# Decayed B and K from a column per chunk, and corner clears and decay diagonals on GpSimd, in a two-layer gated encoder

## The chip, the core and the metric

The kernel runs on one core of a Trainium2 chip. The metric is device time in microseconds from the launch to the end of the program; smaller is better. The core's engines work side by side, each through its own queue in a fixed order: TensorE (PE, with its weight loads as PEld), VectorE (DVE), ScalarE (ACT), GpSimd (POOL), and SyncE (SP), which issues most transfers.

## The reference

Two layers of an encoder with 512 tokens of width 1024 in float32. Each layer projects the normalised input, runs five mixers on parts of the projection, merges their outputs through gates, projects again and normalises. The change lies in one mixer, a recurrence with 8 heads of 64, run forward and backward (e = 0 and 1):

```python
def rwkv7_step(state, inp):
    r, w, k, v, a, bb = inp
    sa = jnp.einsum('bhij,bhj->bhi', state, a)
    state = state * w[:, :, None, :] + sa[..., None] * bb[:, :, None, :] + v[..., None] * k[:, :, None, :]
    return state, jnp.einsum('bhij,bhj->bhi', state, r)
...
    for e, rev in ((0, False), (1, True)):
        ke = k * (1.0 + (a[:, :, e] - 1.0) * k_a)
        be = kk * a[:, :, e]
        xs = (rh, seq_heads(decay[:, :, e]), seq_heads(ke), vh, ah, seq_heads(be))
        _, ye = lax.scan(rwkv7_step, jnp.zeros((b, B_HEADS, HEAD_DIM, HEAD_DIM), F32), xs, reverse=rev)
        ys.append(ye)
```

`decay` is exp of a negative number for each channel and token, so products of decays over a stretch are exp of differences of a running sum.

## The kernel before

**Stages.** An opening part normalises the input. Each layer then has attention mixers, the recurrence, and an end with the last branch of the merge, the output projection and the normalisation. The merge (`branch_steps`, five branches of eight column blocks) consists of long chains of 512-column matmuls. The part of it whose inputs are ready is used as filler: `pull` advances it by one step at each `yield` of the recurrence. Inputs of later branches come back from DRAM into four buffers `o`, by transfers that GpSimd issues (line 366).

**The recurrence** treats the 512 tokens as 8 chunks of 64. A unit is a pair of heads in one direction; there are 8 units in a layer (p = 0 to 3, e = 0 and 1). A unit has an `early` part, which has no link to the state, and a `late` part, which passes the state from chunk to chunk. The loop at the end runs `late` of unit n beside `early` of unit n + 1, and after a pair's backward unit its `finish`.

`early` (line 804 on): a scan (line 820) makes the running sum `csum` of the log decay within each chunk. `tot` is its last column in each chunk, and `gc`, 8 columns, is the decay over a whole chunk. Line 825 makes `bef`, the sum before the token; lines 826 and 827 make `aft`, what remains after it. The forward direction takes `incl, excl, comp` as `csum, bef, aft`, the backward one as their mirror. From the inclusive sum come B and K divided by the decay so far; they lie in `BK` (lines 852 and 853), grouped by halves, and go with A and R into the score matmuls of line 881. Line 908 takes the exponential of `comp`, the decay from a token to its chunk's end. Lines 910 and 912 multiply B (`ai`) and K (`ke`) by it; four transposes each (line 921) and copies by ScalarE (line 927) bring them into `OM`. Line 933 writes, for each head, eight diagonal 64x64 blocks with `gc` on the diagonal into `A0`, the tile named AR (two buffers).

`late` (line 945 on): a 32x32 triangular substitution with 31 steps, each a product `pr` (line 963) and a sum into `W` (line 965) on VectorE, whose result goes into the block-diagonal tile `WD` (line 970). WD has one buffer for all units. Two of its 32x32 corner blocks are left from the unit before, which ran in the other direction; lines 975 and 976 clear them. Lines 981 and 988 fill the other two corners. Then two halves of four chunks follow: line 1009 multiplies WD with Z, line 1024 makes products in PSUM, line 1027 adds the diagonals of A0 and leaves the tile PE, line 1035 starts the outer products, and line 1042 passes the state; between its steps ScalarE and VectorE copy one state quadrant each (lines 1044 and 1045). Lines 1054 and 1055 collect the half's output.

**What sets the order.** The code's order is only a priority. A scheduler that runs when the program is built takes instructions as its own clock makes them ready and fixes each engine's queue; an engine then runs strictly in that order. It also gives out the buffers: the `[128, 512]` tiles of `early` share six under the tag `tmp`. Weights are split into two float32r parts by ScalarE (line 135) and VectorE (line 136) as they come; those operations stand in the same queues.

Of the kernel before, what the change touches and what calls it, by code (L numbers as in the profile page):

```python
# [13 lines left out]
AF = mybir.ActivationFunctionType  # L14
ALU = mybir.AluOpType
# [37 lines left out]
def encoder_kernel(ctx: ExitStack, tc: tile.TileContext, x, mem, ln_in, rel_bias, w_in, par, w_up, a_up,  # L53
                   d_lambda, w_mem, w_branch, w_gate, w_out, lnp, cst, cossin, onehot, cnt, msk, out):
    nc = tc.nc
# [12 lines left out]
    def ps_s():  # L68
        return pp.tile([128, 512], F32, name="psc", tag="psc", bufs=2)
# [11 lines left out]
    act = nc.scalar.activation  # L81
    tt = nc.vector.tensor_tensor
# [189 lines left out]
    with tc.tile_pool(name="init", bufs=1) as ip:  # L272
# [20 lines left out]
        for t in range(2):  # L293
            for j in range(2):
# [4 lines left out]
                sl = slice(t * 128, (t + 1) * 128)  # L299
# [11 lines left out]
        for i in range(2):  # L311
            ps = ps_m()
            sl = slice(i * 512, (i + 1) * 512)
# [10 lines left out]
    for l in range(L):  # L324
# [17 lines left out]
        def finish_o(pool, of, out=False):  # L342

            t = pool.tile([128, 2, S], F32R, name="os", tag="os", bufs=2) if out else new_o()
            split2(t[:, 0, :], t[:, 1, :], of)
            return t
# [64 lines left out]
        with tc.tile_pool(name=f"att{l}", bufs=1) as at:  # L411
# [34 lines left out]
            def softmax(ps, nk, bias=None, norm=DVE):  # L446


                st = tile_of("sst", [128, 4], F32, 16)
                p = tile_of("p", [128, S], F32, 8)[:, :nk]  # L450
                if bias is not None:
                    nc.vector.tensor_tensor_reduce(out=p, in0=ps[:, :nk], in1=bias, scale=1.0, scalar=3.0e38,
                                                   op0=ALU.add, op1=ALU.min, accum_out=st[:, 0:1])
                    src = p
                else:
                    nc.vector.tensor_reduce(out=st[:, 0:1], in_=ps[:, :nk], axis=AX.X, op=ALU.min)
                    src = ps[:, :nk]
                act(p, src, AF.Exp, scale=-1.0, bias=st[:, 0:1], accum_out=st[:, 1:2])
                nc.vector.reciprocal(st[:, 2:3], st[:, 1:2])
                if norm == DVE:  # L460
                    ts(p, p, st[:, 2:3], None, ALU.mult)  # L461
                elif norm == ACT:
                    act(p, p, AF.Copy, scale=st[:, 2:3])
                return p, st
# [30 lines left out]
            def gated(of, g2, out=False):  # L495
                tt(of, of, g2, ALU.mult)
                return finish_o(at, of, out)
# [29 lines left out]
            for hp in range(4):  # L527
# [22 lines left out]
                for i in range(2):  # L550
                    b = load_bias(2 * hp + i)
                    p4 = []
                    for qb in range(4):
                        ps = ps_s()
                        score(ps, q, k, i, qb, S)
                        p, _ = softmax(ps, S, b[:, 384 - 128 * qb:896 - 128 * qb])
# [55 lines left out]
            for b in range(4):  # L612
# [3 lines left out]
                for i in range(2):  # L616
                    p4 = []
                    for qb in range(4):
                        ps = ps_s()
                        score(ps, q, (kh, kl), i, qb, S, g)  # L620
                        p, _ = softmax(ps, S)
# [6 lines left out]
                t = gated(of, g2, True)  # L628
# [8 lines left out]
            with tc.tile_pool(name=f"attd{l}", bufs=1) as ad:  # L637
# [12 lines left out]
                for h in range(4):  # L650
# [25 lines left out]
                    o = ad.tile([128, S], F32, name="oraw", tag="oraw", bufs=2)  # L676
# [7 lines left out]
                    t = finish_o(at, o, True)  # L684
# [3 lines left out]
            for b in range(2):  # L688
# [6 lines left out]
                for i in range(2):  # L695
                    p4 = []
                    for qb in range(4):
                        ps = ps_s()
                        score(ps, q, k, i, qb, 256)
                        p, _ = softmax(ps, 256, None, (DVE, ACT)[qb % 2])  # L700
# [4 lines left out]
                t = gated(of, g2, True)  # L705
# [3 lines left out]
        with tc.tile_pool(name=f"rw{l}", bufs=1) as rp:  # L709
            def T(n, shape, bufs=1, dt=F32):  # L710
                return rp.tile(shape, dt, name=n, tag=n, bufs=bufs)

            def tmp(n="tmp"):
                return rp.tile([128, S], F32, name=n, tag="tmp", bufs=6)

            def recurrence():
# [10 lines left out]
                WD = T("WD", [128, 8, 128])  # L727
# [17 lines left out]
                for b in range(2):  # L745
                    t = tmp()
# [55 lines left out]
                def early(p, e):  # L802
                    if e == 0:
# [6 lines left out]
                    s2 = tmp()  # L810
# [4 lines left out]
                    ai = tmp()  # L815
                    act(ai, ps, AF.Tanh, scale=0.5, bias=cf[:, 22 + i:23 + i])
                    yield
                    hc = 0.5 * CDEC
                    csum = tmp()
                    nc.vector.tensor_tensor_scan(csum, M("rst"), s2, 0.0, ALU.mult, ALU.add)  # L820
                    tot = csum.rearrange("p (c t) -> p c t", t=64)[:, :, 63:64]
                    gc = T("gc", [128, 8], 2)
                    act(gc, tot.rearrange("p c o -> p (c o)"), AF.Exp, scale=-hc)
                    bef = tmp()
                    tt(bef, csum, s2, ALU.subtract)
                    aft = tmp()
                    tt(aft.rearrange("p (c t) -> p c t", t=64), tot.to_broadcast([128, 8, 64]),
                       csum.rearrange("p (c t) -> p c t", t=64), ALU.subtract)
                    if e == 0:
                        incl, excl, comp = csum, bef, aft  # L830
                    else:
                        tt(s2, aft, s2, ALU.add)
                        incl, excl, comp = s2, aft, bef
                    yield

                    ke = tmp()
# [7 lines left out]
                    A0 = T("AR", [128, 8, 3, 64], 2)  # L844

                    def cu(t):
                        return t.rearrange("p (c u t) -> p c u t", u=2, t=64)
# [3 lines left out]
                    bv = BK.rearrange("p c u s t -> p c (u s) t")  # L851
# [10 lines left out]
                    for h in range(2):  # L862
                        sl = slice(64 * h, 64 * h + 64)
# [9 lines left out]
                    for c2 in range(2):  # L873
                        pss = [ps_s(), ps_m()]
                        MB = T("MB", [128, 2, 2, 128], 1)
                        for j in range(4):
                            c = 4 * c2 + j
                            for h, ps in enumerate(pss):
                                sl = slice(64 * h, 64 * h + 64)
                                kb_ = BK[sl, c // 2, c % 2].rearrange("p s t -> p (s t)")  # L880
                                mm(ps[:, j * 128:(j + 1) * 128], kb_, A0[sl, c, 1 - h::1 + h, :], start=True, stop=True)
                        for h, ps in enumerate(pss):
# [4 lines left out]
                            for g in range(4):  # L887
# [3 lines left out]
                                else:  # L891
                                    o = 32 * (1 - e)
# [12 lines left out]
                    q[e] = (Z, NS, OM, A0)  # L905
                    yield

                    act(comp, comp, AF.Exp, scale=-hc)
                    B2, K2 = ai, gx
                    tt(B2, ai, comp, ALU.mult)  # L910
                    for u in range(2):
                        tt(cu(K2)[:, :, u, :], cu(ke)[:, :, 1 - u, :], cu(comp)[:, :, 1 - u, :], ALU.mult)
                    pt = ps_s()
                    for c in range(4):
                        nc.tensor.transpose(pt[:, c * 128:(c + 1) * 128], A[:, c * 128:(c + 1) * 128], ident)
# [13 lines left out]
                    for h in range(2):  # L929
                        sl = slice(64 * h, 64 * h + 64)  # L930
                        idb = ident[sl, 64 * h:64 * h + 64].rearrange("p (o t) -> p o t", o=1).to_broadcast([64, 8, 64])
                        gcb = gc[sl].rearrange("p (c o) -> p c o", o=1).to_broadcast([64, 8, 64])
                        tt(A0[sl, :, h, :], idb, gcb, ALU.mult)
                    if e == 0:
                        nc.vector.tensor_copy(kes, ke)
                    else:
# [8 lines left out]
                def late(p, e):  # L945
                    q = pairs[p]
                    Z, NS, OM, A0 = q[e]
# [25 lines left out]
                    sg = [slice(32 * g, 32 * g + 32) for g in (e, 2 + e)]  # L973
                    tg = [slice(32 * g, 32 * g + 32) for g in (1 - e, 3 - e)]
                    for u in range(2):
                        nc.vector.memset(WD[tg[u], :, sg[u]], 0.0)
                        nc.vector.transpose(out=TN[sg[u]], in_=WD[sg[u], :, sg[u]])
                    ps = ps_t()
                    for k in range(8):
# [115 lines left out]
                pairs = {}  # L1095
                units = [(p, e) for p in range(4) for e in range(2)]
                yield from early(*units[0])
                for n in range(len(units) + 1):
                    live = []
                    if n < len(units):  # L1100
                        live.append(late(*units[n]))
                    if n and units[n - 1][1] == 1:
                        live.append(finish(units[n - 1][0]))
                    if n + 1 < len(units):
                        live.append(early(*units[n + 1]))
                    while live:
                        for g in list(live):
                            if next(g, 0) == 0:
                                live.remove(g)
                            else:  # L1110
                                yield
# [7 lines left out]
        with tc.tile_pool(name=f"out{l}", bufs=1) as op:  # L1119
# [27 lines left out]
            for t in range(4):  # L1147
                sl = slice(t * 128, (t + 1) * 128)
# [131 lines left out]
```

## Time and profile before

| | us |
|---|---|
| median of 3 runs (2258.39 to 2260.19) | 2260.18 |
| the profiled execution | 2261.37 |
| its span, first to last instruction | 2259.6 |
| TensorE busy (share of the span) | 2186.5 (97%) |
| VectorE busy | 1730.6 (77%) |
| ScalarE busy | 1273.2 (56%) |
| GpSimd busy | 59.6 (3%) |
| recurrence of the first layer | 523.6 to about 1030 |
| recurrence of the second layer | 1621 to about 2128 |

Granted TensorE clock: 0.999 of full speed over the span. Busy times count an engine's instructions without waits. A matmul's end is modelled and overlaps the next one's start, so that TensorE may seem busy while it runs late by some tenths of a microsecond. The chain of work that ended last is followed back from the last instruction, at each step to what released it or to the instruction before it on its engine; a piece on it need not be the only cause of the end.

### The profile page before, as it was taken

Reading aid. Unit: us, or ns where it says so; the run is one execution under the profiler, and the core shown is the slowest. Engines: PE = TensorE matmul, PEld = TensorE weight load, DVE = VectorE, ACT = ScalarE, POOL = GpSimd, SP = SyncE. Lnnn points to the kernel's source line nnn. Section 1 sums busy time; section 2 is a strip of 40 time slices with the busy share of each in tenths; the row PEclk is TensorE's granted clock in tenths of the full one; section 3 lists DMA queues with packets and bytes.
Section 4 is the critical chain, followed back from the end, with each engine's and each line's share of the span. In section 5 each row is a group of like instructions: output and inputs, shape, how many; then the busy total and the mean of one; then the engine's idle time right before and its main releaser. Section 6 shows DMA issues by size and latency. Waiting matters only on the chain.

```text
span 2259.6 us, 36239 instructions
## 1 busy us (share of the span) xinstructions
PE 2186.5 (97%) x13056; PEld 1678.6 (74%) x13056; DVE 1730.6 (77%) x4236; ACT 1273.2 (56%) x2785; POOL 59.6 (3%) x117
## 2 busy tenths in 40 slices
PE   6999999999999999999999999999999999999998
PEld 5777777777767777777787777777777777777776
DVE  7677887677989797975568778766788979879565
ACT  3565666676665555644326656677675646565440
POOL 0000000100000000000000000001000000000000
PEclk9999999999999999999999999999999999999999
DMA  7732124322222221315333312333313213222261
GB/s 261 222 108 91 56 80 112 113 86 85 75 80 66 86 88 59 102 49 181 117 115 108 98 62 70 97 106 89 112 57 99 71 62 98 72 80 73 84 195 38
DMA packets 111780, 220.49 MB, mean 98 GB/s; under 512 B 13240, under 2 KB 23224, under 8 KB 111216
## 3 DMA queue, kind: packets, MB, share of 16 engines
q1 hardware_dynamic: 101456, 195.09, 27.0%
q0 software_dynamic: 10144, 23.08, 4.0%
q8 instruction: 103, 1.69, 0.3%
q14 instruction: 77, 0.63, 0.1%
HBM read 187.66 MB, written 27.31 MB: 95 GB/s over the span
## 4 chain that ended last, share of the span: by engine, by line
PE 70%; DVE 14%; ACT 8%; DMA 5%; issue 3%; DVEq 0%; POOL 0%; ACTq 0%; SPq 0%
PE pg L150 10%; PE pg L151 10%; PE pg L149 10%; PE pf L149 6%; PE pf L150 5%; PE pf L151 5%; PE psc L444 4%; PE po L489 3%; PE pt L470 3%; DVE W L965 2%; DVE pr L963 2%; DMA wrawr<-in_w_out_dram 1%; DVE wlof L136 1%; PE po L479 1%; DMA wrawf<-in_w_mem_dram 1%
## 5 line engine op out<-in xcount | busy, mean ns | idle before, releaser
L149 PE MATMUL pg<-hT,whir 128*128 128x512 f32 (+1 forms) x912 | 364.0, 399 | 3.2 <-DVE kl L436 1.4
L150 PE MATMUL pg<-hT,whir 128*128 128x512 f32 (+1 forms) x912 | 365.4, 401 | 0.5 <-DVE hT L176 0.5
L151 PE MATMUL pg<-hT,wlor 128*128 128x512 f32 (+1 forms) x912 | 363.8, 399 | 2.1 <-DVE wlor L136 2.1
L136 DVE TENSOR_TENSOR wlor<-wrawr,whir 128x512 fp32r<-128x512 f32 x240 | 163.9, 688 | 114.8 <-ACT whir L135 104.9
L135 ACT CAST whir<-wrawr 128x512 fp32r<-128x512 f32 x240 | 147.7, 618 | 175.1 <-PE pg L150 116.7
L135 ACT CAST whif<-wrawf 128x512 fp32r<-128x512 f32 (+1 forms) x272 | 164.4, 605 | 135.4 <-PE pf L150 77.9
L149 PE MATMUL pf<-hT,whif 128*128 128x512 f32 x512 | 220.8, 431 | 3.4 <-DVE gt L388 2.8
L136 DVE TENSOR_TENSOR wlof<-wrawf,whif 128x512 fp32r<-128x512 f32 (+1 forms) x272 | 181.4, 669 | 49.2 <-ACT whif L135 43.2
L150 PE MATMUL pf<-hT,whif 128*128 128x512 f32 x512 | 206.7, 404 | 0.0
L151 PE MATMUL pf<-hT,wlof 128*128 128x512 f32 x512 | 205.2, 401 | 0.0
L149 PEld LDWEIGHTS pg<-hT,whir 128*128 128x128 f32 x912 | 172.0, 189 | 40.6 <-issue 3.0
L151 PEld LDWEIGHTS pg<-hT,wlor 128*128 128x128 f32 x912 | 171.9, 188 | 40.0 <-DVE wlor L136 4.9
L150 PEld LDWEIGHTS pg<-hT,whir 128*128 128x128 f32 x912 | 171.9, 189 | 37.8 <-issue 3.9
L176 DVE TENSOR_TENSOR pT<-pt,pT 128x512 fp32r<-128x512 f32 x176 | 114.2, 686 | 34.2 <-ACT pT L175 33.1
L175 ACT CAST pT<-pt 128x512 fp32r<-128x512 f32 x176 | 94.7, 589 | 63.0 <-PE pt L470 61.7
L149 PEld LDWEIGHTS pf<-hT,whif 128*128 128x128 f32 x512 | 96.5, 188 | 35.8 <-DVE gt L388 10.2
L470 PE MATMUL pt<-cst,p 128*128 128x128 f32 x704 | 118.6, 273 | 0.5 <-DVE p L461 0.5
L151 PEld LDWEIGHTS pf<-hT,wlof 128*128 128x128 f32 x512 | 96.4, 188 | 22.2 <-issue 1.6
L963 DVE TENSOR_TENSOR pr<-W,U 128x60 f32<-128x60 f32 (+24 forms) x496 | 103.5, 209 | 11.4
L965 DVE TENSOR_TENSOR W<-W,pr 128x60 f32<-128x60 f32 (+24 forms) x496 | 102.9, 208 | 11.0
L470 PEld LDWEIGHTS pt<-cst,p 128*128 128x128 f32 x704 | 89.8, 141 | 28.4 <-DVE p L461 3.6
L150 PEld LDWEIGHTS pf<-hT,whif 128*128 128x128 f32 x512 | 96.8, 189 | 18.8 <-issue 4.3
(326 smaller groups left out, 4809.1 us busy)
## 6 DMA issues: line engine op xcount, KB each, us to landing
wrawr<-in_w_in_dram SPq DMA_DIRECT2D x224, 256.0 KB, 2.8
wrawf<-in_w_gate_dram SPq DMA_DIRECT2D x160, 256.0 KB, 2.8
o<-scr_o POOLq DMA_DIRECT2D x26, 512.0 KB, 4.5
wrawf<-in_w_branch_dram SPq DMA_DIRECT2D x48, 256.0 KB, 2.7
bias<-scr_toe SPq DMA_DIRECT2D x24, 448.0 KB, 3.3
scr_o<-os SPq DMA_DIRECT2D x20, 512.0 KB, 3.7
wrawf<-in_w_in_dram SPq DMA_DIRECT2D x32, 256.0 KB, 3.0
wrawr<-in_w_out_dram SPq DMA_DIRECT2D x32, 256.0 KB, 2.9
```

Of the source, the lines that this page charges most:

```text
L135: nc.scalar.copy(hi, raw)
L136: tt(lo, raw, f(hi), ALU.subtract)
L149: mm(ps, ah, bh, start=(i == 0), stop=False)
L150: mm(ps, ah, bl, start=False, stop=False)
L151: mm(ps, al, bh, start=False, stop=(i == n - 1))
L175: nc.scalar.copy(hi, src)
L176: tt(lo, src, f(hi), ALU.subtract)
L444: mm(ps[:, :nk], q[:, i, sl], part[:, i if g is None else g, :nk], start=(j == 0), stop=(j == 1))
L470: nc.tensor.transpose(pt[:, qb * 128:(qb + 1) * 128], p4[qb][:, kb * 128:(kb + 1) * 128], ident)
L489: mm(po, vwin(kb), pT[:, b, :], start=(kb == 0 and b == 0), stop=(kb == nkb - 1 and b == 1))
L963: tt(pr, W[:, t8, s:s + 1].to_broadcast([128, nt, n]), U[:, s:s + 1, rsl].to_broadcast([128, nt, n]), ALU.mult)
L965: tt(W[:, t8, rsl], W[:, t8, rsl], pr, ALU.add)
```

## The change

The decay from a token to its chunk's end is the decay over the whole chunk divided by the decay so far. BK already holds B and K divided by the decay so far, so the change multiplies BK by the column `gc` of the chunk, broadcast over 64 tokens. `comp`, its exponential and one of the two differences are not made any more. The clears of WD's corners and the diagonals in A0 are the same operations on GpSimd in place of VectorE. All lines behind 826 move up by one.

```diff
-                    bef = tmp()
-                    tt(bef, csum, s2, ALU.subtract)
-                    aft = tmp()
-                    tt(aft.rearrange("p (c t) -> p c t", t=64), tot.to_broadcast([128, 8, 64]),
-                       csum.rearrange("p (c t) -> p c t", t=64), ALU.subtract)
+                    excl = tmp()
                     if e == 0:
-                        incl, excl, comp = csum, bef, aft
+                        tt(excl, csum, s2, ALU.subtract)
+                        incl = csum
                     else:
-                        tt(s2, aft, s2, ALU.add)
-                        incl, excl, comp = s2, aft, bef
+                        tt(excl.rearrange("p (c t) -> p c t", t=64), tot.to_broadcast([128, 8, 64]),
+                           csum.rearrange("p (c t) -> p c t", t=64), ALU.subtract)
+                        tt(s2, excl, s2, ALU.add)
+                        incl = s2
...
-                    act(comp, comp, AF.Exp, scale=-hc)
                     B2, K2 = ai, gx
-                    tt(B2, ai, comp, ALU.mult)
+                    gcu = gc.rearrange("p (c u o) -> p c u o", u=2, o=1)
+                    tt(cu(B2), bv[:, :, 0::3, :], gcu.to_broadcast([128, 4, 2, 64]), ALU.mult)
                     for u in range(2):
-                        tt(cu(K2)[:, :, u, :], cu(ke)[:, :, 1 - u, :], cu(comp)[:, :, 1 - u, :], ALU.mult)
+                        tt(cu(K2)[:, :, u, :], bv[:, :, 2 - u, :], gcu[:, :, 1 - u, :].to_broadcast([128, 4, 64]), ALU.mult)
...
-                        tt(A0[sl, :, h, :], idb, gcb, ALU.mult)
+                        nc.gpsimd.tensor_tensor(A0[sl, :, h, :], idb, gcb, ALU.mult)
...
-                        nc.vector.memset(WD[tg[u], :, sg[u]], 0.0)
+                        nc.gpsimd.memset(WD[tg[u], :, sg[u]], 0.0)
                         nc.vector.transpose(out=TN[sg[u]], in_=WD[sg[u], :, sg[u]])
```

The order is moved too. In the first layer's second unit (pair 0, backward), VectorE's queue between the output of the first half and the sum PE of the second half was:

```order
L1045 COPY ST_5176<-pt 64x64
L1055 TENSOR_TENSOR SY<-pt,SY 64x256 x2
L965 TENSOR_TENSOR W<-W,pr 128x4x18
L976 MEMSET WD 32x8x32
L963 TENSOR_TENSOR pr<-W,U 128x68
L976 MEMSET WD 32x8x32
L965 TENSOR_TENSOR W<-W,pr 128x4x17
L1027 TENSOR_TENSOR PE<-pt,AR 128x2x128 x2
```

pr, W and U are the substitution's tiles, here those of the next unit; ST is the state, pt the PSUM tile. In the changed program the last ten rows up to the same sum (now line 1026) are:

```order
L962 TENSOR_TENSOR pr<-W,U 128x68
L136 TENSOR_TENSOR wlof<-wrawf,whif 128x512
L964 TENSOR_TENSOR W<-W,pr 128x4x17
L962 TENSOR_TENSOR pr<-W,U 128x64
L964 TENSOR_TENSOR W<-W,pr 128x4x16
L962 TENSOR_TENSOR pr<-W,U 128x75
L964 TENSOR_TENSOR W<-W,pr 128x5x15
L962 TENSOR_TENSOR pr<-W,U 128x70
L964 TENSOR_TENSOR W<-W,pr 128x5x14
L1026 TENSOR_TENSOR PE<-pt,AR 128x2x128 x2
```

The two clears are gone, and the substitution has come to the 128x5x14 step ahead of the sum where it had come to 128x4x17.

GpSimd's queue in the first layer's recurrence was, from the stage's opening clears to the next layer's first key copies:

```order
L728 MEMSET WD 128x1024
L732 MEMSET ST_5175 128x128
L732 MEMSET ST_5176 128x128
L366 DMA o<-scr_o 128x1024 x13
L435 DMA kh<-kh 64x512
```

Its first part is now, up to the clears of unit 4 (units counted from 0):

```order
L975 MEMSET WD 32x8x32 x2
L932 ISA
L932 TENSOR_TENSOR AR<-cst,gc 64x8x64 x4
L975 MEMSET WD 32x8x32 x2
L932 TENSOR_TENSOR AR<-cst,gc 64x8x64 x2
L366 DMA o<-scr_o 128x1024 x4
L975 MEMSET WD 32x8x32 x2
L932 TENSOR_TENSOR AR<-cst,gc 64x8x64 x2
L975 MEMSET WD 32x8x32 x2
L932 TENSOR_TENSOR AR<-cst,gc 64x8x64 x2
L366 DMA o<-scr_o 128x1024 x4
L975 MEMSET WD 32x8x32 x2
```

The 13 reloads of o, which stood together, are now split up by clears (line 975) and diagonals (line 932).

## Rows read from the trace of the kernel before

**Rows 1.** The page: busy us, share of the span and instructions; chain by engine.

```profile
PE 2186.5 (97%) x13056; PEld 1678.6 (74%) x13056; DVE 1730.6 (77%) x4236; ACT 1273.2 (56%) x2785; POOL 59.6 (3%) x117
...
PE 70%; DVE 14%; ACT 8%; DMA 5%; issue 3%; DVEq 0%; POOL 0%; ACTq 0%; SPq 0%
```

**Rows 2.** By stretch: us, busy PE, PEld, DVE, ACT, POOL (instructions), PEclk, DMA, GB/s.

```profile
523.60:1030.00 506.40, 491.69 (x3679) 367.82 (x3678) 418.65 (x1133) 289.83 (x694) 7.21 (x14) 1.00 0.24 75
...
575.00:600.00 25.00, 23.45 (x147) 17.97 (x146) 24.23 (x75) 16.05 (x43) 0.00 (x0) 1.00 0.19 57
```

**Rows 3.** Waits of TensorE's weight loads, 523.6 to 1100 us: in total, times, longest.

```profile
PEld pt L1042 <- DVE ST L1045: 11.9, 29, 0.8
PEld pt L1035 <- DVE PE L1027: 8.1, 12, 1.4
```

**Rows 4.** Groups by line and form, whole span: busy us, mean ns; idle before.

```profile
L933 DVE TENSOR_TENSOR AR<-cst,gc 64x512 f32<-64x512 f32 x32 | 21.9, 684 | 0.5
...
L827 DVE TENSOR_TENSOR tmp<-tmp 128x512 f32<-128x512 f32 x16 | 11.0, 685 | 0.0
...
L852 DVE TENSOR_TENSOR BK<-tmp 128x512 f32<-128x512 f32 x16 | 10.9, 684 | 0.0
...
L976 DVE MEMSET WD<- 32x256 f32 x32 | 8.7, 272 | 3.5 <-POOL WD L728 1.0
...
L908 ACT ACTIVATE tmp<-tmp 128x512 f32<-128x512 f32 x16 | 10.0, 627 | 3.2 <-DVE tmp L825 3.1
```

**Rows 5.** Pieces of the chain in order of time: start us, us, engine and line.

```profile
587.31 0.59 DVE AR L933
...
620.90 0.26 DVE WD L976
...
631.98 0.60 DVE tmp L827
...
798.92 0.10 issue
...
1686.30 0.70 DVE AR L933
...
2026.35 0.28 DVE WD L976
2026.63 0.02 issue
```

**Rows 6.** Timeline, 671.9 to 674 us: start us, us, engine, line, operation, shapes, [idle before].

```profile
671.92 0.23 DVE L963 TENSOR_TENSOR pr<-W,U 128x68 f32<-128x68 f32 x1
...
672.26 0.27 DVE L976 MEMSET WD<- 32x256 f32 x1
...
672.71 0.75 DVE L1027 TENSOR_TENSOR PE<-pt,AR 128x256 f32<-128x256 f32 x2
...
673.18 1.15 PE L1035 MATMUL pt<-UV,OM 128*64 128x64 f32 x32 [0.45 <-DVE PE L1027]
```

**Rows 7.** Timeline where GpSimd computes; of lines 187, 720: ns min/median/max, first, last start.

```profile
21.99 1.85 POOL L321 CAST msk<-mk 128x1152 bf16<-128x1152 f32 x1 [21.55 <-DMA mk<-in_msk_dram]
...
22.77 1.11 DVE L187 TENSOR_SCALAR rsy<-lnmv 128x2 int32<-128x2 int32 x1
...
L187 DVE TENSOR_SCALAR rsy<-lnmv x8: 145/156/1106, 8.6 to 2253.2; 128x2 int32<-128x2 int32 x4, 128x1 int32<-128x1 int32 x4
...
1621.37 0.99 POOL L728 MEMSET WD<- 128x1024 f32 x1 [56.03 <-DVE cf L719]
...
L720 DVE TENSOR_SCALAR cf<-cf x2: 168/590/1011, 523.3 to 1621.4; 128x14 f32<-128x14 f32 x2
...
1621.60 0.82 DVE L725 TENSOR_SCALAR cf<-par 128x4 f32<-128x4 f32 x1
```

**Rows 8.** Timeline: second reloads of o on GpSimd, and line 1009 of unit 4.

```profile
786.33 0.54 POOL L366 DMA_DIRECT2D o<-scr_o  x1 [150.72 <-PE pf L151]
...
843.40 1.05 PE L1009 MATMUL pt<-Z,WD 128*128 128x128 f32 x8
```

## The prediction

> **What bounds the kernel now.** I read the page's busy shares and chain first, then busy time by stage, then who waits for whom on TensorE in the recurrence, and at last single pieces of the chain. TensorE is busy 97% of the span of 2259.6 us and makes 70% of the chain; VectorE is busy 77% and makes 14% [rows 1]. The profiled execution took 2261.37 us, 1.2 us above the median of 2260.18 us; I sum against the profile and take 1.2 us off at the end.
>
> The change lies wholly in the two recurrences, one per layer, each about 506 us long. There TensorE's order is fixed when the program is built: short matmuls of the recurrence stand between 512-column ones of the gated merge, so a late result of VectorE stops the filler too. VectorE is the near-bound: 418.65 us of 506.40, and 24.23 us of 25 where a unit's early part and another's late part coincide [rows 2]. TensorE's longest waits there are on VectorE: in one layer 11.9 us for the state copies and 8.1 us for the sum PE of line 1027 [rows 3]. Both are small; 20 us a layer is about what VectorE could give back by those two waits.
>
> **What leaves VectorE and ScalarE.** There are 16 units (4 pairs, 2 directions, 2 layers). Each drops one 128x512 difference (line 827 in the forward direction, 825 in the backward), two clears of 32x256 and two diagonals of 64x512, and ScalarE drops one Exp. From the rows by form [rows 4]: 16 x 0.685 = 11.0 us, 32 x 0.272 = 8.7 us, 32 x 0.684 = 21.9 us; together 41.6 us of VectorE's 1730.6. ScalarE loses 16 x 0.627 = 10.0 us. The three products that make B and K keep their count and size; the row of line 852, which already walks BK in that strided pattern, costs the same 684 ns as a plain one [rows 4], so reading BK and a broadcast column I cost at nothing extra. BK has one buffer and is now read later, but by VectorE itself, which writes the next unit's BK after that in its own order; no wait is added.
>
> **What of it lies on the path.** Only what stands on the chain can bring time.
> - Clears: 25 of the 32 are on the chain, first (after one at the stage's start) at 620.90 and last at 2026.35 us, 0.26 to 0.28 us each; in six of a layer's eight units both are. Before one there is 0.10 us of issue where other pairs show 0.02 [rows 5]. The reason is in the timeline: the clear may go only when the unit before has left WD, which is just when that unit's second half wants PE. In the second unit two clears, the later at 672.26 us, stand ahead of the sum of line 1027 at 672.71, and TensorE idles 0.45 us before line 1035 for that sum [rows 6]. 24 x (0.28 + 0.10) = 9.1 us is the most that they give.
> - But the order shows that the slots don't stay empty. Where the clears stood, the changed program puts more steps of the substitution (pr and W, 0.23 us the one in [rows 6]) in front of the sum. The last nine rows ahead of it hold eight such steps and a weight remainder. So the sum can again be late, only the substitution is further. I take half: -4.6 us; bounds 0 and -9.1.
> - Diagonals: 4 of 32 are on the chain, two in each layer (the first at 587.31, 0.59 us; the last 0.70 us) [rows 5]: -2.6 us.
> - Differences: of the dropped ones 2 are on the chain, 0.60 us each (the first at 631.98) [rows 5]: -1.2 us.
> - Exp: none of the 16 is on the chain; it precedes products that are now ready sooner, and TensorE's transposes of them lie in filler. I take -1.0 us; bounds 0 and -1.8 us, its 10.0 us at the 18% of VectorE's busy time that the chain holds (14% of 2259.6 over 1730.6) [rows 1].
>
> **What comes back from GpSimd.** No row shows GpSimd doing a product, so I bound it. A GpSimd clear of 1024 columns took 0.99 us, which makes 512 columns 0.5 us; a cast of 1152 columns took 1.85 us [rows 7]. But the same rows show that the two engines stop each other. The cast began while VectorE was in a 128x1024 operation; the next VectorE instruction, a two-element one that takes 0.16 us otherwise (median), took 1.11 us and ended with the cast. In the second layer four tiny VectorE operations that began beside GpSimd's clear, at 0.01 to 0.23 us from its start, all ended with it, one after 1.01 us where its twin in the first layer took 0.17 us [rows 7]. So VectorE may lose what the GpSimd product holds. The cast behind the other engine's operation ran about 1.07 us (22.77 to 23.84 us), 0.93 ns a column; two operands of 512 columns at that pace are 0.95 us. I take 0.95 us a product, bounds 0 (it meets an operation that doesn't want the same path) and 1.85 us.
>
> The diagonals will run as soon as gc is there, so amid the unit's own early products, where VectorE is fullest. I charge the four that were on the chain: 4 x 0.95 = +3.8 us against the 2.6 us saved. The other 28 I cost at nothing: the same work was off the chain before (684 ns each), and a block of 0.95 us is 0.27 us more. Their cover is the early part's lead of about one unit; if that cover is gone, they are the third rival below. The clears on GpSimd are 0.3 us by the 0.99 us row and meet mostly products.
>
> The Trainium skill (SBUF — State Buffer, Who interferes with whom) says that a VectorE instruction with two SBUF inputs contends with a GpSimd instruction that reads SBUF, not with one that only writes, and that the first comer holds the path for its whole instruction. This speaks against the diagonals and for the clears; the cast agrees, the tiny operations beside the clear were not products. Its GPSIMD Engine Reference (Elementwise — side-by-side cycle accounting) has 4497 ns for 2048 columns; a quarter, as an estimate, is 1.12 us, by which the four would return 4.5 instead of 3.8 us.
>
> **Queues.** GpSimd's queue carried only reloads of o in this stage, waiting up to 150.72 us for a merge branch to end [rows 8]. Now clears and diagonals stand between them. A clear behind a waiting reload would hold TensorE's line 1009. In the order the second four reloads stand ahead of unit 4's clears; they began at 786.33 us and the first of those clears at 799.02 (behind the 0.10 us of issue at 798.92), while line 1009 of that unit, which reads WD, came at 843.40 [rows 5, 8]. I cost it at nothing. The waits that are added (line 1009 and ScalarE's WD copy on GpSimd) are for clears made a unit's half earlier.
>
> **Sum.** -4.6 - 2.6 + 3.8 - 1.2 - 1.0 = -5.6 us: 2255.8 us for a profiled execution, **2254.6 us** as a median, 0.25% faster. About 0.2% (4.5 us) is what a measurement of this kernel can tell from no change, so this forecast lies close to that line.
>
> **Rivals.**
> - *Everything saved counts.* The clears give 9.1, diagonals 2.6 and nothing returns, differences 1.2, Exp 1.8: -14.7 us, 2245.5 us. For it: VectorE at 24 of 25 us. Against: the refilled slots and [rows 7].
> - *The slots refill wholly.* TensorE's order keeps the same distance from line 1024 to 1035, VectorE reaches the sum as late as before, and diagonals return what they save: -1 to -2 us, about 2259. For it: TensorE at 97% with the same matmuls. Against: 41.6 us of work is really gone from the engine that is waited for.
> - *The path between the two engines.* In the early part, from the scan to BK, GpSimd's products stop VectorE for the cast's 1.85 us each: 32 x 1.85 = 59.2 us lost for 41.6 saved, 17.6 us more. If 30% of it reaches the end (18% is VectorE's mean on the chain, the clears have 25 of 32), that is +5.3 us: 2265.5 us, slower. It decides from a mean stop of 41.6/32 = 1.3 us. For it: [rows 7]. Against: many VectorE operations read PSUM or run off the chain. The skill's 1.12 us estimate lies under that point.
> - *It doesn't do what it says*: a clear stuck behind a reload, stopping line 1009 by several us in some units. The 44 us between clear and reader speak against it; it would end near 2265 too.
>
> **Numbers.** Forecast (2250 to 2255.7) 0.36; all saved (below 2250) 0.14; refilled or just short of the line (2255.7 to 2264.7) 0.33; engines' path 0.14 and stuck clears 0.03, above 2264.7. So faster 0.50, same 0.33, slower 0.17. The range from 2246 to 2264 leaves about 0.18 out.
>
> **What would show it.** Right: VectorE's busy time down by 20 to 42 us with GpSimd's up by 40 to 60; no clear of VectorE on the chain; TensorE's wait for line 1027's successor (8.1 us a layer before) down to some 5. Small VectorE operations, or products, of 1 us and more beside a GpSimd product would show the stops; I expect them at unit 1 of each layer. Wrong: the wait for the state copies (11.9 us) grown, TensorE waiting for GpSimd at line 1009, or VectorE's operations uniformly slower.

## The result, and the profile after

The changed kernel took 2272.47 us (median of 4 runs, 2271.2 to 2273.05) against 2259.28 before (4 runs): ratio 1.0056, 95% interval 1.0044 to 1.0068. It is 13 us slower; 2254.6 was forecast, in a range to 2264. The profiled execution took 2272.89 us.

The page of the changed kernel, with the rows that answer to [rows 1]:

```profile
span 2271.1 us, 36306 instructions
...
PE 2185.2 (96%) x13056; PEld 1681.3 (74%) x13056; DVE 1724.3 (76%) x4156; ACT 1263.7 (56%) x2769; POOL 107.6 (5%) x181
...
PE 69%; DVE 19%; ACT 6%; issue 3%; DMA 3%; DVEq 0%; ACTq 0%; SPq 0%
```

VectorE has 80 instructions less and was to lose 20 to 42 us; its busy time fell by 6.3. Its share of the chain rose from 14 to 19%. ScalarE lost the 10 us of the Exps and GpSimd gained 48 us, as worked out. So the instructions left, and most of their time came back in longer ones. Which ones, the timeline shows where GpSimd makes the two diagonals of the fourth unit of layer 1 (start, us, engine, line, operation):

```profile
681.36 0.69 DVE L829 TENSOR_TENSOR tmp<-tmp 128x512 f32<-128x512 f32 x1
681.97 1.53 DVE L136 TENSOR_TENSOR wlof<-wrawf,whif 128x512 fp32r<-128x512 f32 x1
683.42 1.53 DVE L831 TENSOR_TENSOR tmp<-tmp 128x512 f32<-128x512 f32 x1
684.88 0.54 DVE L836 TENSOR_SCALAR tmp<-tmp,cf 128x512 f32<-128x512 f32 x1
...
681.78 2.62 POOL L932 TENSOR_TENSOR AR<-cst,gc 64x512 f32<-64x512 f32 x2 [11.78 <-ACT gc L823]
```

Line 829 began ahead of GpSimd and took its 0.69 us. The next two, beside the products, took 1.53 us, 0.84 us more each. Line 836, behind them, took its usual 0.54. All 32 products start as soon as `gc` is there, so right behind the scan. The rows by line (ns min/median/max, first and last start):

```profile
L932 POOL TENSOR_TENSOR AR<-cst,gc x32: 1040/1168/1440, 552.2 to 2048.9; 64x512 f32<-64x512 f32 x32
...
L836 DVE TENSOR_SCALAR tmp<-tmp,cf x16: 533/1268/1414, 552.7 to 2050.5; 128x512 f32<-128x512 f32 x16
...
L831 DVE TENSOR_TENSOR tmp<-tmp x8: 679/1530/1532, 574.3 to 2049.0; 128x512 f32<-128x512 f32 x8
  ACT tmp L849: 20.3, 8
...
L975 POOL MEMSET WD<- x32: 301/304/308, 523.1 to 2096.8; 32x256 f32 x32
```

10 of the 16 instructions of line 836 and 6 of the 8 of line 831 are stretched; taking `pr` and the weight remainder of line 136 with them, every unit has two stretched ones, by 0.5 to 0.9 us. Line 831 is a step from the scan to `BK`; ScalarE's line 849 waited 20.3 us for it (6.7 us in the kernel below that clears in place of the products). What then comes late is seen in TensorE's waits, 523.6 to 1100 us (in total, times, longest), which answer to [rows 3]; the last two lines are of the kernel before:

```profile
PEld pt L1041 <- DVE ST L1044: 13.0, 28, 2.3
PEld pf L149 <- ACT gt L380: 12.2, 19, 2.3
PEld pt L1034 <- DVE PE L1026: 7.0, 9, 1.3
PEld pf L149 <- DVE gt L388: 6.9, 12, 1.4
...
PEld pf L149 <- ACT gt L380: 7.6, 17, 1.0
PEld pf L149 <- DVE gt L388: 5.1, 12, 1.1
```

The wait for the sum PE fell from 8.1 to 7.0, less than the 5 that I had looked for; the one for the state copies rose from 11.9 to 13.0, with a longest of 2.3 in place of 0.8. Most of what was added is in the filler's waits (line 149) for `gt`, 12.2 for 7.6 and 6.9 for 5.1. The loss builds up inside the two recurrences: the changed kernel is 1.8 us ahead where the first one clears WD (line 728, 521.82 against 523.60 us), 4.5 us behind where the second one does (1625.84 against 1621.37) and 11.5 us behind at the end of the span.

### The profile page after: what moved, and what is told of

The parts are those of the page before. It is cut to its first block, busy times and chain, and to the rows that moved or that the text cites. A ratio compares the mean times of both kernels' runs of the same rounds, so it can differ in the third digit from the quotient of the medians.

```text
span 2271.1 us, 36306 instructions
## 1 busy us (share of the span) xinstructions
PE 2185.2 (96%) x13056; PEld 1681.3 (74%) x13056; DVE 1724.3 (76%) x4156; ACT 1263.7 (56%) x2769; POOL 107.6 (5%) x181
## 4 chain that ended last, share of the span: by engine, by line
PE 69%; DVE 19%; ACT 6%; issue 3%; DMA 3%; DVEq 0%; ACTq 0%; SPq 0%
PE pg L151 10%; PE pg L150 10%; PE pg L149 10%; PE pf L149 5%; PE psc L444 4%; PE pf L150 4%; PE pf L151 4%; PE po L489 3%; PE pt L470 3%; DVE pr L962 2%; DVE wlof L136 2%; DVE W L964 2%; PE pt L1034 1%; PE po L479 1%; PE psc L151 1%
## 5 line engine op out<-in xcount | busy, mean ns | idle before, releaser
L136 DVE TENSOR_TENSOR wlof<-wrawf,whif 128x512 fp32r<-128x512 f32 (+1 forms) x272 | 190.9, 703 | 48.5 <-ACT whif L135 41.6
L149 PEld LDWEIGHTS pf<-hT,whif 128*128 128x128 f32 x512 | 96.6, 189 | 40.4 <-DVE gt L388 13.8
L962 DVE TENSOR_TENSOR pr<-W,U 128x60 f32<-128x60 f32 (+24 forms) x496 | 106.9, 216 | 12.4
L149 PE MATMUL pf<-o,whif 128*128 128x512 f32 x224 | 99.1, 442 | 13.4 <-ACT gt L380 13.4
```

The lines of the kernel that those rows point to most:

```text
L136: tt(lo, raw, f(hi), ALU.subtract)
L149: mm(ps, ah, bh, start=(i == 0), stop=False)
L962: tt(pr, W[:, t8, s:s + 1].to_broadcast([128, nt, n]), U[:, s:s + 1, rsl].to_broadcast([128, nt, n]), ALU.mult)
```

## Experiments

Theory A: GpSimd's products stop VectorE amid the chain from the scan to BK; the rest of the change is harmless. Rivals: the new order (B), any work of GpSimd there (C), the clears' waits (D). A ratio is against the kernel before, run on the same chip.

### One part at a time

The changed kernel with the diagonals back on VectorE:

```diff
-                        nc.gpsimd.tensor_tensor(A0[sl, :, h, :], idb, gcb, ALU.mult)
+                        tt(A0[sl, :, h, :], idb, gcb, ALU.mult)
```

> The changed kernel with the diagonals back on VectorE; the clears stay on GpSimd. Theory A: 32 x 0.684 = 21.9 us return to VectorE, 32 stops of 0.84 us = 27 us go, and the early part's products take 0.69 us again: 2254 to 2260, no slower than the kernel before. Theory B (order): 2265 or more, since nearly all of the new order stays. Theory D (the clears' waits between the engines cost it): 2265 or more, with TensorE or ScalarE waiting for GpSimd's clears.

2247.26 us, 0.9941 (0.9929 to 0.9954): 25 us below the changed kernel, faster than the kernel before, and 7 us below theory A's own range, as the algebra gives more than I had (next). D falls. So does B for the order that the two kernels share; the clearing kernels below, with the changed kernel's order on VectorE, test it better.

The same with the clears on VectorE too, so the algebra alone:

```diff
-                        nc.gpsimd.memset(WD[tg[u], :, sg[u]], 0.0)
+                        nc.vector.memset(WD[tg[u], :, sg[u]], 0.0)
```

> The new form of the products alone: clears and diagonals both on VectorE, as in the kernel before; 16 differences and 16 Exp fewer. Theory A: 2255 to 2259, a little faster than the kernel before or the same (differences 1.2 us and Exp 1.0 us by the forecast). Theory B (the reordering that comes with the algebra costs): above 2264. If it is faster than the kernel with the clears on GpSimd, the clears cost; if slower, they gain: the forecast had 4.6 us for them.

2247.83 us, 0.9947 (0.9935 to 0.996): 12.6 us faster than before, where I had 2.2. So the clears add 0.6 us here, which the runs don't resolve. The kernel before with the clears alone on GpSimd (that line the other way):

> The kernel before with the clears alone on GpSimd. Theory A with the forecast's term: 2259.3 - 4.6 = 2254.7, bounds 2250 and 2259. Theory D (waits on GpSimd's clears cost): above 2262, with TensorE's line 1009 or ScalarE's WD copy waiting for GpSimd. VectorE's busy time falls by 32 x 0.272 = 8.7 us in either.

2257.87 us, 0.9987 (0.9979 to 0.9996): 2.5 us faster, inside the forecast's bounds for the term. VectorE's busy time fell by 3.4 us (1730.6 to 1727.2), not by 8.7. And the kernel before with the diagonals alone on GpSimd:

> The kernel before with the diagonals alone on GpSimd. Theory A: 24 us more than the kernel before, whatever form the other products have: 2280 to 2290. Rival (only with the algebra's shorter chain do the products meet the early products): 2258 to 2270.

2279.83 us, 1.0088 (1.0075 to 1.0102): 20 us slower, without the algebra, at the lower edge of theory A's range. Put on one after the other the parts are -12.6, -0.6 and +25.2, which is the whole by construction. Each alone on the kernel before they are -12.6, -2.5 and +19.7, together +4.5 where the change costs 12 to 13: the same diagonals cost 5 us more on top of the algebra. No run here shows why.

### What in the product costs

The product replaced by a clearing, and by a copy of the identity:

```diff
-                        nc.gpsimd.tensor_tensor(A0[sl, :, h, :], idb, gcb, ALU.mult)
+                        nc.gpsimd.memset(A0[sl, :, h, :], 0.0)
...
+                        nc.gpsimd.tensor_copy(A0[sl, :, h, :], idb)
```

> The changed kernel, with GpSimd's two diagonal products per unit replaced by its clearing of the same 64x512 block; so the decay of the state across a chunk is left out of what is computed. Order and count of the instructions on every engine stay those of the changed kernel. Theory A (the products' reads stop VectorE, 0.84 us each, 27 us in all): the stretched 128x512 products beside them (1.53 us) are back at 0.69, VectorE's busy time falls by some 27 us to about 1697, the time falls to 2254 to 2260. Theory B (the changed order of the instructions costs the time, the stops are covered): within 4 us of the changed kernel, 2268 to 2273, though VectorE is quicker. Theory C (any work of GpSimd at that place stops VectorE): the stretches stay, at 2268 to 2273.

> The changed kernel with GpSimd's two products per unit replaced by a copy of the identity into the same 64x512 block, so one operand read instead of two (the decay of the state is left out of what is computed); same order and count of instructions as the changed kernel on every engine. Theory A1 (any GpSimd instruction that reads beside a VectorE product stops it): VectorE's 128x512 products beside it are stretched by about the copy's length, 0.5 to 0.9 us, and the time stays at 2264 to 2273. Theory A2 (only a second operand read stops): no stretch, about 2248 as with the clearing in its place.

2248.59 us (0.9942, 0.9928 to 0.9956) and 2255.37 us (0.9977, 0.9968 to 0.9986). The first lies below theory A's range, the second between A1 and A2. That seemed to settle it, but neither waits for `gc`: their traces show them earlier, beside the substitution, where a copy stretched `pr` and `W` by some 0.4 us. So the place had changed as well. A small GpSimd copy of `gc` ahead of them was to hold them back, in two kernels:

> The changed kernel with each unit's two GpSimd products replaced by a small GpSimd copy of gc (128x8) and, behind it in GpSimd's queue, the clearing of the same two 64x512 blocks, so that GpSimd writes them at the place where the products stood, right behind gc (the decay of the state is left out of what is computed). TensorE's order differs from the changed kernel's in 18 of 8170 rows. Theory A (the products' reads stop VectorE): no 128x512 operation beside the clearing takes over 0.7 us; 2247 to 2252, the small copy costing at most its own length. Rival W (the place is what costs: GpSimd's wait for gc, or any work of GpSimd amid the early chain): 2262 to 2273.

> As the kernel with the clearing at the products' place, but with a copy of the identity into the two blocks (one operand read; the decay left out here too); same order. Theory A: a copy of 0.61 us stops VectorE by about 0.4 us, as it did beside the substitution, but here amid the early chain: 32 x 0.4 = 13 us, at nearly full price, 2256 to 2264. Rival W: like the clearing there, whatever that gives.

2246.53 us (0.9937, 0.992 to 0.9953) and 2254.13 us (0.9973, 0.9962 to 0.9983), but the scheduler put the clearing and the copy back beside the substitution; only the small copy stood at the products' place. So these two can't decide between A and W. They repeat the first two (7.6 us between them, with 8.6 us of VectorE, rows below), and show that a wait of GpSimd for `gc` by itself costs nothing. Then both were tied by data: one operand read from `gc`, or a small copy into the same block and the clearing over it:

```diff
-                        nc.gpsimd.tensor_tensor(A0[sl, :, h, :], idb, gcb, ALU.mult)
+                        nc.gpsimd.tensor_scalar(A0[sl, :, h, :], gcb, 0.0, None, ALU.mult)
...
+                        nc.gpsimd.tensor_copy(A0[sl, 0, h, 0:8], gc[sl])
+                        nc.gpsimd.memset(A0[sl, :, h, :], 0.0)
```

> The changed kernel with GpSimd's diagonal products replaced by gc times the constant zero into the same 64x512 blocks: one operand read instead of two, behind gc as the products are, with the same order on every engine (the decay of the state is left out of what is computed). Theory A (a GpSimd read beside a VectorE operation stops it, by about the GpSimd operation's length): stops of 0.4 to 0.85 us, 32 of them 13 to 27 us, at the place where the products' 25 us of stops cost 25: 2258 to 2273. Theory A2 (only the read of the identity stops, or only two operands): 2246 to 2250. Rival W (the place or the wait for gc costs): 2262 to 2273 without stretched operations.

> The changed kernel with each product replaced by a small GpSimd copy of gc (64x8) into the block and the clearing of the whole block behind it, which the small copy holds at the products' place, right behind gc (the decay of the state is left out). TensorE's order differs from the changed kernel's in 18 of 8170 rows. Theory A (reads stop, writes don't): the 64x512 clearings stretch nothing, the small copies by at most their 0.33 us in some of 32 places: 2246 to 2254. Rival W (any work of GpSimd amid the early chain, or its wait for gc): 2262 to 2273.

2258.13 us (0.999, 0.998 to 0.9999) and 2245.71 us (0.9937, 0.9922 to 0.9952), the first at the lower edge of theory A's range, the second 0.3 us below it. The same unit in the kernel that clears at the products' place:

```profile
677.58 0.68 DVE L136 TENSOR_TENSOR wlof<-wrawf,whif 128x512 fp32r<-128x512 f32 x1
678.19 0.68 DVE L831 TENSOR_TENSOR tmp<-tmp 128x512 f32<-128x512 f32 x1
678.79 0.54 DVE L836 TENSOR_SCALAR tmp<-tmp,cf 128x512 f32<-128x512 f32 x1
...
677.38 0.94 POOL L932 COPY AR<-gc 64x8 f32<-64x8 f32 x2 [11.75 <-ACT gc L823]
678.38 1.42 POOL L933 MEMSET AR<- 64x512 f32 x2
```

GpSimd works there nearly as long as with the products (2.36 against 2.62 us), and nothing on VectorE is stretched. With one operand read:

```profile
681.10 1.09 DVE L136 TENSOR_TENSOR wlof<-wrawf,whif 128x512 fp32r<-128x512 f32 x1
682.12 0.68 DVE L831 TENSOR_TENSOR tmp<-tmp 128x512 f32<-128x512 f32 x1
682.72 0.83 DVE L836 TENSOR_SCALAR tmp<-tmp,cf 128x512 f32<-128x512 f32 x1
...
680.93 3.22 POOL L932 TENSOR_SCALAR AR<-gc 64x512 f32<-64x512 f32 x2 [11.78 <-ACT gc L823]
```

The operation lasts longer (1.6 us) and stops less (0.3 to 0.4 us each). B, C and W fall: VectorE's order is the changed kernel's in both, instruction for instruction, and the clearing at the same place costs nothing, so it is the reads. Last, the products made twice, in nearly the same order:

```diff
+                        for _ in range(2):
+                            nc.gpsimd.tensor_tensor(A0[sl, :, h, :], idb, gcb, ALU.mult)
```

> The changed kernel with each GpSimd diagonal product made twice, 64 in place of 32. Theory A: the stops double; 32 of them cost 2272.5 - 2248.6 = 23.9 us against clearing in their place, so 2290 to 2300. Rival (the cost comes from the TensorE clock's drops or from one wait per unit that the first product makes, not from the sum of stops): 2272 to 2280.

2309.95 us, 1.0221 (1.0207 to 1.0235). The rows of the pages with the clearing, with one operand read and with the products twice follow in this order; the one with the products stands with the result:

```profile
PE 2174.6 (97%) x13056; PEld 1674.5 (75%) x13056; DVE 1697.5 (76%) x4156; ACT 1265.4 (56%) x2769; POOL 101.1 (5%) x213
```

```profile
PE 2181.7 (97%) x13056; PEld 1678.8 (74%) x13056; DVE 1711.2 (76%) x4156; ACT 1265.4 (56%) x2769; POOL 123.0 (5%) x181
```

```profile
PE 2201.8 (95%) x13056; PEld 1691.6 (73%) x13056; DVE 1751.4 (76%) x4156; ACT 1264.6 (55%) x2769; POOL 150.9 (7%) x213
```

VectorE has the same 4156 instructions in the same order in all four, so what its busy time grows by are the stops:

| at the products' place | VectorE busy | stops | time | more time |
|---|---|---|---|---|
| clearing | 1697.5 | 0 | 2245.71 | 0 |
| one operand read | 1711.2 | 13.7 | 2258.13 | 12.4 |
| products (changed kernel) | 1724.3 | 26.8 | 2272.47 | 26.8 |
| products twice | 1751.4 | 53.9 | 2309.95 | 64.2 |

By the ratios, each against the kernel before on its chip, the last column is 12.0, 26.9 and 64.2. A microsecond of stop costs a microsecond of time, the last row more (2309.95 is above theory A's range too). The Trainium skill (SBUF — State Buffer, Who interferes with whom) says that a GpSimd instruction that reads SBUF contends with a VectorE one that has two SBUF inputs, and one that only writes does not. These rows agree: 0.68 beside the clearing, 1.53 us beside the product. Line 836 goes beyond that rule as told: it reads one tile and columns of `cf`, and was stretched from 0.54 to 1.27 us (median) beside the product and not beside the clearing; no run here shows why. And that the first comer holds the path for its whole instruction, as the prediction has it, isn't so with one operand read: line 136 ended at 682.19, while the operation of 1.6 us that had begun at 680.93 still ran.

### Does the place matter?

The products held back until K is made:

```diff
+                    gcl = T("gcl", [128, 8], 2)
+                    stt(gcl, K2[:, 0:8], 0.0, gc, ALU.mult, ALU.add)
...
-                        gcb = gc[sl].rearrange("p (c o) -> p c o", o=1).to_broadcast([64, 8, 64])
+                        gcb = gcl[sl].rearrange("p (c o) -> p c o", o=1).to_broadcast([64, 8, 64])
```

> The changed kernel with GpSimd's diagonal products held back until the unit's K product is made: they read a copy of gc that a small VectorE operation (128x8, 0.16 us, 16 of them = 2.6 us) makes behind K. Same 32 products of GpSimd, so the same stops, but behind the chain from the scan to K. Theory A-place (a microsecond of VectorE counts fully only between the scan and the products of BK, A and r; behind them it has slack, as the diagonals on VectorE had: 21.9 us at no cost): 2248 to 2258. Theory A-sum (a stop costs its length wherever it falls): 2268 to 2275.

2264.07 us, 1.002 (1.0011 to 1.0028): between the two, so neither theory as it stood, and 16.8 us above the diagonals on VectorE. The rows of the pages, with the diagonals on VectorE, with the products held back, and of the two kernels above with the clearing and the copy beside the substitution:

```profile
PE 2177.3 (97%) x13056; PEld 1676.0 (75%) x13056; DVE 1716.8 (76%) x4188; ACT 1266.4 (56%) x2769; POOL 69.2 (3%) x149
...
PE 2184.0 (97%) x13056; PEld 1678.6 (74%) x13056; DVE 1717.9 (76%) x4172; ACT 1266.1 (56%) x2769; POOL 114.5 (5%) x181
...
PE 2176.7 (97%) x13056; PEld 1675.9 (75%) x13056; DVE 1699.1 (76%) x4156; ACT 1264.6 (56%) x2769; POOL 92.2 (4%) x197
...
PE 2176.5 (97%) x13056; PEld 1675.2 (74%) x13056; DVE 1707.7 (76%) x4156; ACT 1264.6 (56%) x2769; POOL 97.8 (4%) x197
```

The first two keep VectorE equally long, 1716.8 and 1717.9 us. So VectorE's own diagonals cost next to nothing (2247.26 against 2245.71 with the clearing, for 19.3 us of VectorE), while stops cost nearly their length even late (18.4 us over the clearing, for 20.4 us of VectorE, 2.5 of them the small operation's; TensorE's granted clock was 0.51 for 6.8 us of the second recurrence, from 2008.8 us on, which is at most 3.4 of the 18.4). Beside the substitution, in the late part, the copy's stops cost 7.6 us for 8.6 us of VectorE, in the same order on every engine. So a stop costs most of its length in all three places. What waits with the products held back (layer 1, 523.6 to 1100 us) is another matmul:

```profile
PE pm L92 <- DVE OM L895: 4.5, 5, 1.5
```

The likely reason why VectorE's own diagonals are cheap is the order: the scheduler lays it with the diagonals' time in it and puts them where VectorE has room, but its order is the same row for row for the product and for the one-operand form, so it plans no stop, and a stop holds whatever stands next. That is argued; no run shows it.

### Where the algebra's 12.6 us come from

The algebra alone with the difference made again, and with the Exp made again, into a tile that nobody reads:

```diff
+                        dmy = T("dmy", [128, S])
+                        tt(dmy, csum, s2, ALU.subtract)
...
+                    dmy = T("dmy", [128, S])
+                    act(dmy, nkk, AF.Exp, scale=-hc)
```

> The new form of the products alone, with the dropped 128x512 difference made again in its old place into a buffer that nobody reads; the Exp stays dropped. The algebra alone ran at 2247.8 us against 2260.4 before, 12.6 us, where the chain held 1.2 us of the differences. Theory P (an operation between the scan and BK is on the path in every unit): the 16 x 0.685 = 11.0 us of VectorE come back in full, 2256 to 2260. Theory Q (the Exp in front of B and K was on the path): stays at 2247 to 2251. Theory R (sixth temporary buffer: one temporary less per unit frees the rotation): stays at 2247 to 2251, and the kernel with the Exp added stays there too.

> The new form of the products alone, with one 128x512 Exp of ScalarE per unit in the old place, into a buffer that nobody reads. Theory P (difference in the early chain): stays at 2247 to 2251, since the products don't wait for this Exp. Theory Q' (ScalarE's 0.627 us itself delays the copies behind it): 2253 to 2258. What neither this nor the added difference brings back belongs to the products' wait for the Exp, or to the temporary buffers.

2261.85 us (1.0008, 0.9999 to 1.0016) and 2249.68 us (0.9954, 0.9942 to 0.9967). The 11.0 us of differences bring back 14.0 us, all of the gain and more than their length; the Exp brings back up to 2 us, which the runs don't resolve. The added tile takes none of the six `tmp` buffers, and the time came back all the same, so buffers are not the cause. With the difference the scheduler's order goes back nearly to that of before; how much is the operation's length and how much the order, these runs don't separate.

### Is there more to have?

One WD for each direction, so no clears at all, with the diagonals on VectorE; and that with one step of the early chain on ScalarE:

```diff
-                WD = T("WD", [128, 8, 128])
-                nc.gpsimd.memset(WD, 0.0)
+                WDS = [T("WD%d" % d, [128, 8, 128]) for d in range(2)]
...
-                        nc.gpsimd.memset(WD[tg[u], :, sg[u]], 0.0)
...
-                    ts(ai, ai, -0.5, -0.5, ALU.mult, ALU.add)
+                    act(ai, ai, AF.Copy, scale=-0.5, bias=-0.5)
```

> The new form of the products, diagonals on VectorE, and one WD for each direction, so that its cleared corners stay clear and the 32 clears of the recurrences are gone from every engine. Theory A (what stands in VectorE's row between a unit's halves is on the path): against the algebra alone (2247.8 us) it saves 32 x 0.272 = 8.7 us of VectorE and also the wait for the last reader of the one WD; as the move of the clears to GpSimd alone gave 0.6 to 2.5 us, 2243 to 2248. If the shared WD held units apart, more: below 2243.

> The kernel with one WD per direction, and one more operation taken off the chain between scan and BK: the scale and shift of ai (128x512, a VectorE TENSOR_SCALAR of 0.43 us with its row of 16) goes to ScalarE. Theory P (VectorE's work between the scan and BK counts in full): 16 x 0.43 = 6.9 us, 2246.2 - 6.9 = 2239.3, from 2237 to 2243. Rival S (ScalarE's 0.6 us and the way there and back stand on the same chain, or delay gt and the Exps): 2244 to 2252.

2246.21 us (0.9938, 0.9924 to 0.9952) and 2247.13 us (0.9948, 0.9934 to 0.9961). The first is as fast as the kernel with the clears on GpSimd; both beat the kernel before by 13 to 15 us and the changed one by 25 to 26. The second gained nothing, where 6.9 us were expected: VectorE's busy time fell from 1717.3 to 1710.1 us, but the wait of line 149's weight loads for ScalarE's `gt` grew from 7.1 to 9.5 us in layer 1 (523.6 to 1033 us).

## Why the prediction was wrong

- **Diagonals, +1.2 forecast (-2.6 saved, +3.8 back), +25.2 measured.** This is the step that failed. The mechanism was right, and its size nearly: 0.95 us a product was taken, it lasted 1.17 (median) and stopped VectorE by 0.84. But I charged four products, and of the others the prediction says "The other 28 I cost at nothing", since the same work had been off the chain on VectorE. A stop isn't the work that it replaces. VectorE's own diagonals cost 1.6 us, all 32; GpSimd's stopped whatever stood next in VectorE's fixed order, in every unit, and 26.8 us of stops cost 26.8 us. The cover, the early part's lead of about one unit, isn't there for a stop. The prediction names the place, "amid the unit's own early products", but place is the smaller part: held back behind K the products still cost 16.8 us.
- **The third rival** was the case, at a wrong price. It decided from a mean stop of 1.3 us, counting the 41.6 us saved like the stops and 30% of both. In truth the 21.9 us of diagonals saved gave next to nothing (1.6 us), the 11 us of differences, with the order that came with them, all, the stops all: 0.84 us was enough.
- **Differences, -1.2 forecast, about -11 to -12 measured.** I took the 2 of 16 that the chain of waits held. One chain shows what ended last, not what else would have come earlier: each unit has a difference between scan and BK. That each counted by its length is not shown, as the order changed with them.
- **Clears, -4.6 forecast:** -2.5 on the kernel before, -0.6 (not resolved) on the algebra. The doubt about refilled slots was right and half of 9.1 still too much.
- **Exp, -1.0 forecast:** up to -1.9, not resolved. **Queues, 0:** right; no clear was held behind a reload, and no row of GpSimd is on the chain.
- **What was to show it.** VectorE's busy time was to fall by 20 to 42 us and fell by 6. Even without stops it falls by 33.1 (1730.6 to 1697.5), not by 41.6: VectorE's records overlap (line 829 above begins at 681.36 and takes 0.69 us, the next begins at 681.97), so their lengths added up are too much. Operations of 1 us and more beside GpSimd's products stand in every unit, not in unit 1 alone; the state copies' wait grew. No clear of VectorE is on the chain, which was right and worth little.

## To carry to other kernels

Before work goes to GpSimd, see whether it reads SBUF and what VectorE does at the moment when it will start: beside VectorE's 128x512 operations a write was free here (tiny ones beside a 128x1024 clear were held, [rows 7]), while a read cost its stop nearly in full wherever it fell, though the same work on VectorE had cost next to nothing. Price a stop at its length, in every unit, and not by how many operations of the kind one chain of waits happens to hold.

## What the hardware showed beyond that

TensorE's clock fell to its lower level where the stops left it idle. In the changed kernel, by stretch (us; busy PE, PEld, DVE, ACT, POOL with instructions; granted clock, DMA, GB/s):

```profile
946.30:949.90 3.60, 1.69 (x6) 0.72 (x6) 3.60 (x7) 2.45 (x5) 0.00 (x0) 1.00 0.00 0
949.90:953.30 3.40, 3.40 (x10) 2.62 (x9) 2.98 (x7) 2.79 (x4) 0.00 (x0) 0.50 0.14 39
953.30:956.70 3.40, 3.40 (x16) 2.77 (x15) 3.32 (x9) 2.56 (x5) 0.00 (x0) 1.00 0.26 77
```

TensorE waited 1.91 us for line 1073's square, late from VectorE's stretched row, and then ran at 1.2 GHz until 953.3: 10 matmuls where 16 follow at 2.4 GHz. There are three such stretches in the two recurrences, none in those of the kernel before; at 1.7 us each they are at most 5 of the 25 us, and the one-operand kernel, which has no such stretch there, lost its 12.4 us all the same. With the products twice the mean was 0.988 (changed kernel 0.996), which goes with its 64 us for 54 us of stops.
